# A hybrid decoder block on one core: memory keys ahead of the block, memory values inside its first feed-forward step, the memory output projection in token halves

## The chip, the cores and the metric

One core of a Trainium2 chip runs the whole kernel. The metric is device time in microseconds (us), median of several runs. Every matrix product outside the score and transpose steps is the sum of three fp32r products of operands split into a high and a low part.

## The reference

Sequence 1024, width 1024, feed-forward width 2816, 256 memory tokens, one layer.

```python
x = x + 0.5 * swiglu(rmsnorm(x, ffn1_norm), ffn1_w_gate, ffn1_w_up, ffn1_w_down)
x = x + hybrid_mixer(rmsnorm(x, mix_norm), ...)          # NSA and forgetting attention
x = x + memory_cross_attention(rmsnorm(x, mem_q_norm), rmsnorm(mem, mem_kv_norm), mem_w_q, mem_w_kv, mem_w_o)
x = x + 0.5 * swiglu(rmsnorm(x, ffn2_norm), ffn2_w_gate, ffn2_w_up, ffn2_w_down)
return rmsnorm(x, final_norm)
```

In the memory attention, `k, v = split(mem_n @ w_kv)`: keys and values depend on the memory alone, not on x. Its last step is `o @ w_o`.

## The kernel before

**The plan.** The kernel first describes all its work as operations with the engines that could do them and a cost in ns for each, and then `Plan.order` lays them out in one list: at each step it takes the engine on which something can start first and, among the operations that can start there within 60 ns of that, the one of lowest rank. An operation that names two engines goes to the one that is free first by the plan. The order in which operations come out is the order of each engine's instruction stream, and an engine takes its stream strictly in that order. So a cost in the plan changes no instruction; it changes what stands behind what. A rank is roughly the due time in us of TensorE's work (`self.r` grows by the cost of each TensorE operation); loads are ranked some us ahead of their use. Buffers come from shared pools (46 of 128x1024 in SBUF, 8 PSUM banks) with a cap per kind (`TAGS`: F 28, mT 4, raw weight sums' input wa 4, wf 6, results sg 4, vt 2, raw weight units wr 3, their two parts w 10, xs 3); the plan holds an operation back until a buffer is free by its own clock.

**Start.** `memory_kv` norms the two memory tiles (`norm_T`, buffers mT), then makes the eight key blocks (`keys`: one weight unit w each, one 256-column product in cc, stored to DRAM) and the two value halves (`values`: four weight units each, 512-column products, stored). A weight unit comes by DMA (wr), ScalarE casts its high part (L409), VectorE makes its low part (L413). All of it comes ahead of the first feed-forward step. The eight tiles of x (128 tokens each, tokens of the second half first: `late`) are normed at ranks 6 to 34 (`norm_forms`), between the keys and the values.

**A feed-forward step** uses a seven-product scheme for a two by two split of tokens and width (Winograd's). `Forms` holds the seven combinations of the normed, transposed x, each as high and low part (F). `norm_forms` norms a tile (square on ScalarE, reciprocal root on GpSimd, scale on VectorE in xn, L444), transposes it on TensorE (T, L381), copies it out (R for tokens of the second half, xs for the first, at most three xs at once), sums the parts a form needs (fs, L492, on GpSimd or VectorE) and splits it (L390 high, L397 low). Which form needs which (width half, token half) is said by

```python
SUMS = {1: ((0, 0), (1, 1), 1), 2: ((0, 0),), 3: ((0, 1), (1, 1), -1), 4: ((1, 0), (0, 0), -1), 5: ((1, 1),),
        6: ((0, 0), (0, 1), 1), 7: ((1, 0), (1, 1), 1)}
```

so forms 3 and 5 need tokens of the second half alone, 4 and 2 of the first half alone, and 1, 6 and 7 of both. `seven` makes the products in the order 3, 5, 4, 2, 1, 6, 7, each of 12 matmuls over 512 columns; `ffn_up` calls it for gate and up in each of 11 chunks, `left_sums` makes the weight sums (ws) and their split (wf). `ffn_down` follows.

**Second entry.** `out_proj("mo", ..., late=True)` makes the memory output projection for each half of the width (ch), and within it for all eight token tiles, second half first. Only with ch 1 is a tile of x complete: the add (L1327), then `done(t)`, which stores x and calls `norm_forms` for the second feed-forward step. A tile takes eight operations of 648 ns and two of 436 of TensorE's by the plan, so tiles stand 6.06 ranks apart.

## Time and profile before

| | us |
|---|---|
| median of 3 runs | 2586.99 (2584.11 to 2588.99) |
| profiled execution, its own time | 2588.4 |
| span of the trace in it | 2586.4 |
| TensorE busy | 2522.5 |
| VectorE busy | 1664.6 |
| ScalarE busy | 1180.9 |
| GpSimd busy | 619.3 |

The profiled execution is 1.4 us above the median, and 2.0 us of its time lie outside the span. Busy time is the union of an engine's instructions; times in rows are us from the start of the span, means of one instruction are ns.

### The profile page before, as it was taken

What the parts mean: (1) busy time and instruction counts of PE and PEld (TensorE: products, weight loads), DVE (VectorE), ACT (ScalarE), POOL (GpSimd) and SP (SyncE); (2) the same over time, 40 slices, a digit from 0 to 9 for tenths busy, and PEclk for the clock granted to TensorE, in tenths of its full rate; (3) what the DMA queues carried; (4) which work ended last, traced back from release to release, by engine and by line L of the source; (5) the groups of instructions that cost most, each with busy time, mean ns of one, the idle gap of its engine ahead of it and who ended that gap; (6) DMA issues with size and microseconds to landing.
All of it is one profiled execution on the core that took longest, in us unless ns stands there. A gap on an engine that the chain in (4) does not pass through costs nothing.

```text
span 2586.4 us, 34955 instructions
## 1 busy us (share of the span) xinstructions
PE 2522.5 (98%) x12613; PEld 2132.7 (82%) x12613; DVE 1664.6 (64%) x3120; ACT 1180.9 (46%) x2352; POOL 619.3 (24%) x590
## 2 busy tenths in 40 slices
PE   7899999999999999999999999999998999999998
PEld 6688888888788888898888888888876888888887
DVE  8755556667765477788766766344576556557566
ACT  6422232334445567777776753233443232233433
POOL 5643344331200001111000003000034334332313
PEclk9999999999999999999999999999998999999999
DMA  7233233696722110210212344241112223327964
GB/s 280 98 114 114 78 131 118 205 369 225 266 82 83 45 58 30 72 63 19 79 53 82 116 137 155 82 147 57 50 74 86 97 103 106 123 93 271 343 234 164
DMA packets 137485, 329.90 MB, mean 128 GB/s; under 512 B 14656, under 2 KB 18096, under 8 KB 137184
## 3 DMA queue, kind: packets, MB, share of 16 engines
q1 hardware_dynamic: 137248, 327.47, 36.5%
q8 instruction: 99, 1.62, 0.3%
q14 instruction: 74, 0.61, 0.1%
q0 software_dynamic: 64, 0.20, 0.0%
HBM read 254.17 MB, written 75.02 MB: 127 GB/s over the span
## 4 chain that ended last, share of the span: by engine, by line
PE 89%; DVE 3%; ACT 2%; DMA 1%; issue 1%; POOL 0%; SPq 0%; DVEq 0%; POOLq 0%; ACTq 0%
PE z L375 11%; PE z L376 11%; PE z L377 11%; PE mm L375 7%; PE mm L376 7%; PE mm L377 7%; PE y L376 5%; PE y L375 5%; PE y L377 5%; PE T L381 4%; PE pv L1124 4%; PE acc L377 2%; PE acc L375 2%; PE acc L376 2%; PE s L1049 2%; PE s L1050 2%
## 5 line engine op out<-in xcount | busy, mean ns | idle before, releaser
L375 PE MATMUL z<-F,wf 128*128 128x512 f32 x1232 | 483.1, 392 | 15.0 <-ACT wf L513 5.0
L377 PE MATMUL z<-F,wf 128*128 128x512 f32 x1232 | 482.0, 391 | 3.5 <-DVE wf L514 3.5
L376 PE MATMUL z<-F,wf 128*128 128x512 f32 x1232 | 482.6, 392 | 2.5 <-DVE F L397 2.4
L492 POOL TENSOR_TENSOR ws<-wa 128x512 f32<-128x512 f32 x197 | 285.7, 1465 | 507.6 <-DVE wf L514 333.6
L375 PEld LDWEIGHTS z<-F,wf 128*128 128x128 f32 x1232 | 232.8, 189 | 66.7 <-ACT wf L513 5.5
L375 PE MATMUL mm<-h,w 128*128 128x512 f32 x704 | 286.8, 407 | 0.0
L377 PE MATMUL mm<-h,w 128*128 128x512 f32 x704 | 276.5, 393 | 0.0
L376 PE MATMUL mm<-h,w 128*128 128x512 f32 x704 | 276.4, 393 | 0.0
L377 PEld LDWEIGHTS z<-F,wf 128*128 128x128 f32 x1232 | 232.7, 189 | 52.7 <-DVE wf L514 4.6
L376 PEld LDWEIGHTS z<-F,wf 128*128 128x128 f32 x1232 | 232.8, 189 | 52.2 <-DVE F L397 4.0
L376 PE MATMUL y<-df,gf 128*128 128x512 f32 x616 | 239.9, 389 | 1.1 <-DVE df L649 1.1
L375 PE MATMUL y<-df,gf 128*128 128x512 f32 x616 | 240.4, 390 | 0.0
L377 PE MATMUL y<-df,gf 128*128 128x512 f32 x616 | 239.9, 389 | 0.0
L514 DVE TENSOR_TENSOR wf<-ws,wf 128x512 fp32r<-128x512 f32 x220 | 170.7, 777 | 48.8 <-ACT wf L513 48.8
L397 DVE TENSOR_TENSOR pt<-T,pt 128x512 fp32r<-128x512 f32 (+1 forms) x264 | 156.2, 614 | 68.4 <-ACT pt L390 67.3
L390 ACT CAST pt<-T 128x512 fp32r<-128x512 f32 (+1 forms) x264 | 132.3, 528 | 77.5 <-PE T L381 75.5
L1077 ACT ACTIVATE p<-p,sm 128x128 f32<-128x128 f32 (+7 forms) x192 | 143.4, 747 | 46.3 <-DVE sm L1147 43.8
L377 PEld LDWEIGHTS mm<-h,w 128*128 128x128 f32 x704 | 132.6, 188 | 29.7
L513 ACT CAST wf<-ws 128x512 fp32r<-128x512 f32 x220 | 131.8, 619 | 47.4 <-PE z L377 45.5
L376 PEld LDWEIGHTS mm<-h,w 128*128 128x128 f32 x704 | 133.6, 190 | 18.8
L375 PEld LDWEIGHTS mm<-h,w 128*128 128x128 f32 x704 | 133.3, 189 | 19.0
L413 DVE TENSOR_TENSOR w<-wr,w 128x1024 fp32r<-128x1024 f32 x95 | 121.4, 1289 | 40.4 <-ACT w L409 38.7
(254 smaller groups left out, 5042.3 us busy)
## 6 DMA issues: line engine op xcount, KB each, us to landing
da<-in_w_dram SPq DMA_DIRECT2D x264, 256.0 KB, 5.9
wr<-in_w_dram SPq DMA_DIRECT2D x95, 512.0 KB, 4.7
wa<-in_w_dram SPq DMA_DIRECT2D x88, 512.0 KB, 3.9
dg<-gd SPq DMA_DIRECT2D x70, 512.0 KB, 6.0
gd<-gs SPq DMA_DIRECT2D x110, 256.0 KB, 2.1
xd<-x SPq DMA_DIRECT2D x24, 512.0 KB, 2.6
x<-xd SPq DMA_DIRECT2D x24, 512.0 KB, 5.9
gd<-sg SPq DMA_DIRECT2D x44, 256.0 KB, 2.1
```

What stands on the lines that cost most here:

```text
L375: mm(out, a[0], b[0], start=first, stop=False, skip_group_check=more)
L376: mm(out, a[0], b[1], start=False, stop=False, skip_group_check=more)
L377: mm(out, a[1], b[0], start=False, stop=last, skip_group_check=more)
L381: self.nc.tensor.transpose(out, src, self.ident[0:k, 0:k])
L390: nc.scalar.copy(h, s)
L397: nc.vector.tensor_sub(l, s, h.bitcast(F32))
L413: self.dve(1135, lambda: nc.vector.tensor_sub(lo(), raw(), hi().bitcast(F32)), [raw, hi], [lo], rank=r + 4)
L492: (nc.vector if en == "DVE" else nc.gpsimd).tensor_tensor(out(), a(), b(), op=op)
L513: self.act(512, lambda: nc.scalar.copy(w()[:, 0:512], val()), rd, [(w, 0)], sbuf=True, rank=rank + 3)
L514: self.dve(690, lambda: nc.vector.tensor_sub(w()[:, 512:1024], val(), w()[:, 0:512].bitcast(F32)), rd + [(w, 0)], [(w, 1)], rank=rank + 3)
L1077: nc.scalar.activation(p[e]()[:, 0:row[e]], p[e]()[:, 0:row[e]], AF.Exp, bias=m[e]()[:, j:j + 1], scale=-1.0, accum_out=l()[:, e:e + 1])
L1124: mm(pv()[:, 0:256], v, y()[:, b * 256:b * 256 + 256], start=unit["fresh"], stop=stop and y is lo)
```

## The change

It has five parts.

1. At the start the memory keys come first (ranks from -20), the loads and norms of x move forward among them (loads at ranks -13 to -2.5, norms at 3j-2), and the two value halves are moved into `ffn_up`, ahead of its third and fourth chunk. The low part of a key's weight unit may be made by VectorE or by GpSimd.
2. In `norm_forms` the sums and splits of forms 1, 6 and 7 get a rank 14 later (`WAIT`), in both feed-forward steps.
3. `out_proj("mo")` goes by token halves: tokens of the second half with both width halves, then tokens of the first half with both. The eight weight units are loaded and split twice.
4. In `norm_T` and `norm_forms` the plan counts the scale of a tile (xn) as ready 1000 ns later than it costs.
5. The plan's costs of VectorE operations on 512 columns go down from 690 to 603 ns (of `sum_on` and of the splits in `ffn_down` by 87 ns).

```diff
         if pool:
-            self.pool(2430, lambda: nc.gpsimd.tensor_sub(lo(), raw(), hi().bitcast(F32)), [raw, hi], [lo], rank=r + 4)
+            self.plan.op({"DVE": 1135, "POOL": 3000}, lambda en: (nc.vector if en == "DVE" else nc.gpsimd).tensor_sub(
+                lo(), raw(), hi().bitcast(F32)), [raw, hi], [lo], r + 4)
...
-            self.dve(1.042 * n + 130, scale, [x, st, g], [(out, key(j))])
+            self.dve(1.042 * n + 130, scale, [x, st, g], [(out, key(j))], delay=slack)
...
-        self.rms(x, g, xn)
+        self.rms(x, g, xn, slack=1000.0)
...
-        self.plan.op({"POOL": 2.9 * n + 50, "DVE": 1.04 * n + 157}, f, reads, writes, self.r if rank is None else rank)
+        self.plan.op({"POOL": 2.9 * n + 50, "DVE": 1.04 * n + 70}, f, reads, writes, self.r if rank is None else rank)
...
-            self.dve(690, lambda: nc.vector.tensor_sub(w()[:, 512:1024], val(), w()[:, 0:512].bitcast(F32)),
+            self.dve(603, lambda: nc.vector.tensor_sub(w()[:, 512:1024], val(), w()[:, 0:512].bitcast(F32)),
...
         for i in (5, 3) if half else (4, 2, 1, 6, 7):
-            parts = F.SUMS[i]
+            parts, rank = F.SUMS[i], self.r + (WAIT if i in (1, 6, 7) else 0.0)
...
-    def ffn_up(self, n, F):
+    def ffn_up(self, n, F, between={}):
...
         for c in range(H):
+            between.get(c, lambda: None)()
             sg = [self.buf("sg") for _ in range(2)]
...
-        g = self.gain("mem_kv_norm")
+        g = self.gain("mem_kv_norm", lead + 0.5)
...
-            w, ps, kt = self.weight(("mk", c)), self.buf("mm"), self.buf("cc", F32R)
+            w, ps, kt = self.weight(("mk", c), pool=True), self.buf("mm"), self.buf("cc", F32R)
...
-    def out_proj(self, name, y, x, done, late=False):
+    def out_proj(self, name, y, x, done, halves=(range(NT),)):
...
-        for ch in range(2):
+        for ts, ch in ((ts, ch) for ts in halves for ch in range(2)):
             ws = [self.weight((name, ch, j), 16.0 - 4 * j) for j in range(4)]
-            for t in [4, 5, 6, 7, 0, 1, 2, 3] if late else range(NT):
+            for t in ts:
...
-        for f in self.memory_kv(40.0):
+        self.r = -20.0
+        keys = self.memory_kv(0.0)
+        values = [keys.pop(), keys.pop()][::-1]
+        self.r = 0.0
+        for f in keys:
             f()
-        r = self.r
-        self.r = 2.0
-        g = self.gain("ffn1_norm", 0.0)
-        x = load(lambda t: io["x"][t], order=late, lead=2.0, step=2.0)
+        r, self.r = self.r, -13.0
+        g = self.gain("ffn1_norm", 0.5)
+        x = load(lambda t: io["x"][t], order=late, lead=0.0, step=1.5)
         F = Forms(self, "F")
         for j, t in enumerate(late):
-            self.r = 6.0 + 4.0 * j
+            self.r = 3.0 * j - 2.0
             self.norm_forms(x[t], g, F, t)
...
-        gd = self.ffn_up("1", F)
+        gd = self.ffn_up("1", F, {2: values[0], 3: values[1]})
...
-        self.out_proj("mo", o, x, done, late=True)
+        self.out_proj("mo", o, x, done, (late[:4], late[4:]))
...
-G0 = 3
+G0, WAIT = 3, 14.0
```

## Rows read from the trace of the kernel before

**Rows 1.** The page: span, busy time of TensorE (PE), and its granted clock in 40 slices of 64.7 us (tenths of full speed).

```profile
span 2586.4 us, 34955 instructions
...
PE 2522.5 (98%) x12613; PEld 2132.7 (82%) x12613; DVE 1664.6 (64%) x3120; ACT 1180.9 (46%) x2352; POOL 619.3 (24%) x590
...
PEclk9999999999999999999999999999998999999999
```

**Rows 2.** Who waited for whom, TensorE's waits alone, over the whole span (us in total, times, longest).

```profile
PE T L381 <- DVE xn L444: 26.0, 7, 8.1
PE z L375 <- ACT wf L513: 5.0, 1, 5.0
PE z L375 <- ACT vt L537: 4.3, 2, 3.7
```

**Rows 3.** Busy time of each engine in stretches of the start (us; in brackets the number of instructions; then granted clock, share of the DMA engines, GB/s).

```profile
0.00:18.30 18.30, 3.58 (x16) 3.18 (x17) 8.88 (x13) 10.16 (x17) 5.49 (x13) 1.00 0.91 339
18.30:60.00 41.70, 41.53 (x290) 38.94 (x288) 38.55 (x55) 32.73 (x69) 22.59 (x19) 1.00 0.76 271
60.00:110.00 50.00, 34.09 (x133) 26.22 (x134) 44.15 (x60) 26.02 (x59) 37.95 (x23) 0.90 0.29 102
```

**Rows 4.** Instructions of TensorE in order of time, first 110 us, those that waited longest (start us, us, line, what, count; in brackets the idle time before and what ended it).

```profile
16.68 1.97 PE L381 MATMUL T<-ident,xn 128*128 128x128 f32 x8 [6.61 <-DVE xn L444]
...
63.54 1.78 PE L381 MATMUL T<-ident,xn 128*128 128x128 f32 x8 [3.58 <-DVE xn L444]
79.68 1.94 PE L381 MATMUL T<-ident,xn 128*128 128x128 f32 x8 [5.22 <-DVE xn L444]
...
105.25 0.51 PE L375 MATMUL z<-F,wf 128*128 128x512 f32 x1 [2.02 <-DVE vt L541]
```

**Rows 5.** Groups of TensorE's instructions, first 110 us (busy us, mean ns of one | idle before). The memory keys are mm<-mT,w, the memory values mm<-w,mT, the feed-forward products z<-F,wf, the transposes of a normed tile T<-ident,xn; of the three lines L375, L376 and L377 of one product the first is shown.

```profile
L375 PE MATMUL mm<-mT,w 128*128 128x256 f32 x64 | 19.4, 303 | 0.0
L375 PE MATMUL mm<-w,mT 128*128 128x512 f32 x32 | 14.1, 439 | 0.0
L381 PE MATMUL T<-ident,xn 128*128 128x128 f32 x80 | 13.9, 331 | 23.5 <-DVE xn L444 23.5
L375 PE MATMUL z<-F,wf 128*128 128x512 f32 x23 | 9.4, 407 | 3.1 <-DVE vt L541 2.0 <-ACT vt L537 0.7 <-ACT F L390 0.4
```

**Rows 6.** Groups of VectorE's (DVE) instructions, first 105 us (busy us, mean ns of one | idle before).

```profile
L397 DVE TENSOR_TENSOR F<-fs,F 128x256 fp32r<-128x256 f32 x40 | 25.9, 700 | 1.6 <-ACT F L390 1.6
L413 DVE TENSOR_TENSOR w<-wr,w 128x1024 fp32r<-128x1024 f32 x16 | 21.9, 1381 | 2.9 <-ACT w L409 2.9
L444 DVE SCALAR_TENSOR_TENSOR xn<-x,sm,gain 128x1024 f32<-128x1024 f32 x8 | 13.6, 1702 | 0.0
L397 DVE TENSOR_TENSOR cc<-mm,cc 128x256 fp32r<-128x256 f32 (+1 forms) x11 | 5.3, 486 | 1.4 <-ACT cc L390 1.4
```

**Rows 7.** Busy time of each engine in two stretches at the entry to the second feed-forward step (columns as in group 3).

```profile
1927.80:1962.00 34.20, 20.36 (x64) 14.80 (x62) 26.61 (x44) 16.54 (x42) 18.00 (x13) 0.75 0.17 62
1962.00:1996.00 34.00, 34.00 (x152) 28.15 (x151) 22.07 (x30) 9.06 (x17) 9.75 (x8) 1.00 0.26 89
```

**Rows 8.** Instructions of TensorE in order of time at the same place, those that waited.

```profile
1934.46 0.80 PE L375 MATMUL z<-F,wf 128*128 128x512 f32 x1 [3.67 <-ACT vt L537]
1944.00 0.80 PE L375 MATMUL z<-F,wf 128*128 128x512 f32 x1 [5.03 <-ACT wf L513]
1952.94 0.50 PE L375 MATMUL z<-F,wf 128*128 128x512 f32 x1 [3.23 <-ACT F L390]
1955.25 0.80 PE L376 MATMUL z<-F,wf 128*128 128x512 f32 x1 [1.80 <-DVE F L397]
```

**Rows 9.** Instructions of VectorE in order of time: the last split of a form at the start, and then at the second entry.

```profile
95.83 2.47 DVE L397 TENSOR_TENSOR F<-fs,F 128x256 fp32r<-128x256 f32 x2 [1.62 <-ACT F L390]
...
1925.90 6.06 DVE L397 TENSOR_TENSOR F<-fs,F 128x256 fp32r<-128x256 f32 x8
...
1938.53 2.76 DVE L397 TENSOR_TENSOR F<-fs,F 128x256 fp32r<-128x256 f32 x8
1941.22 0.68 DVE L1327 TENSOR_TENSOR x<-acc,x 128x512 f32<-128x512 f32 x1
...
1944.59 1.28 DVE L444 SCALAR_TENSOR_TENSOR xn<-x,sm,gain 128x1024 f32<-128x1024 f32 x1
```

**Rows 10.** Instructions of GpSimd (POOL) in order of time at the same place.

```profile
1924.87 2.27 POOL L492 TENSOR_TENSOR fs<-xs,R 128x512 f32<-128x512 f32 x1 [0.66 <-DVE F L397]
1927.84 1.42 POOL L492 TENSOR_TENSOR fs<-xs,R 128x512 f32<-128x512 f32 x1 [0.70 <-DVE F L397]
1929.61 1.40 POOL L492 TENSOR_TENSOR fs<-xs 128x512 f32<-128x512 f32 x1 [0.36 <-DVE F L397]
```

**Rows 11.** Busy time of each engine in a dense stretch of the first feed-forward step.

```profile
250.00:300.00 50.00, 50.00 (x222) 41.39 (x222) 28.47 (x41) 15.43 (x29) 23.20 (x16) 1.00 0.34 121
```

**Rows 12.** Busy time of each engine while the memory output projection runs, and TensorE's only wait of that stretch.

```profile
1840.00:1889.00 49.00, 48.44 (x219) 39.96 (x218) 16.20 (x18) 8.27 (x11) 2.04 (x3) 1.00 0.06 22
...
1888.05 1.09 PE L381 MATMUL T<-ident,xn 128*128 128x128 f32 x8 [0.56 <-DVE xn L444]
```

**Rows 13.** Groups over the whole span with shapes kept apart: a subtraction or sum of 128x1024 on GpSimd, and the cast of a weight unit on ScalarE (ACT).

```profile
L409 ACT CAST w<-wr 128x1024 fp32r<-128x1024 f32 x95 | 98.9, 1053 | 79.2 <-PE acc L377 53.0 <-DMA wr<-in_w_dram 15.3 <-DVE w L413 6.7
...
L492 POOL TENSOR_TENSOR da<-da 128x1024 f32<-128x1024 f32 x24 | 66.0, 2750 | 178.7 <-DMA da<-in_w_dram 114.9 <-DVE df L649 46.6 <-PE z L376 8.7
```

More of the change, by code (lines that the diff above doesn't have):

```diff
@@ L360, in act, with dve @@
                      hold=hold)
-    def dve(self, ns, run, reads, writes, rank=None):
-        self.plan.op({"DVE": ns}, lambda _: run(), reads, writes, self.r if rank is None else rank)
+    def dve(self, ns, run, reads, writes, rank=None, delay=0.0):
+        self.plan.op({"DVE": ns}, lambda _: run(), reads, writes, self.r if rank is None else rank, delay)
     def pool(self, ns, run, reads, writes, rank=None):
@@ L421, in gain, with rms @@
         return g
-    def rms(self, x, g, out, parts=1):
+    def rms(self, x, g, out, parts=1, slack=0.0):
         nc, n = self.nc, D // parts
@@ L540, in seven @@
         product(4, y, True)
-        self.dve(690, lambda: nc.vector.tensor_add(v(), y(), v()), [y], [(vt, 0)])
+        self.dve(603, lambda: nc.vector.tensor_add(v(), y(), v()), [y], [(vt, 0)])
         product(2, y, False)
@@ L544, in seven @@
         product(1, x, True)
-        self.dve(690, lambda: nc.vector.tensor_add(v(), x(), v()), [x], [(vt, 0)])
+        self.dve(603, lambda: nc.vector.tensor_add(v(), x(), v()), [x], [(vt, 0)])
         product(6, y, False)
-        self.dve(690, lambda: sub(d, y), [y, (vt, 0)], [(vt, 1)])
+        self.dve(603, lambda: sub(d, y), [y, (vt, 0)], [(vt, 1)])
         use(1, 1, d, [(vt, 1)])
         product(7, z, False)
-        self.dve(690, lambda: sub(v, z), [z], [(vt, 0)])
+        self.dve(603, lambda: sub(v, z), [z], [(vt, 0)])
         use(0, 0, v, [(vt, 0)])
@@ L556, in norm_forms @@
         xn = self.buf("xn")
-        self.rms(x, g, xn)
+        self.rms(x, g, xn, slack=1000.0)
         raw = F.raw[t] = self.buf("R" if half else "xs")
@@ L577, in norm_forms @@
                 s = self.buf("fs")
-                self.sum_on(512, s, lambda parts=parts: part(parts[0]), lambda parts=parts: part(parts[1]), parts[2], src, [s])
+                self.sum_on(512, s, lambda parts=parts: part(parts[0]), lambda parts=parts: part(parts[1]), parts[2], src, [s], rank)
                 val, rd = s, [s]
@@ L582, in norm_forms @@
             self.split(512, view, lambda p=put: p(0), lambda p=put: p(1), rd, [(b, t % 4) for b in F.t[i][0]],
-                       [(b, t % 4) for b in F.t[i][1]], count=2, sbuf=True)
-    def ffn_up(self, n, F):
+                       [(b, t % 4) for b in F.t[i][1]], count=2, sbuf=True, rank=rank)
+    def ffn_up(self, n, F, between={}):
         nc, H = self.nc, NFF // 2
@@ L598, in up @@
             def up(i, j, view, reads, sg=sg, at=at):
-                self.dve(690, lambda: nc.vector.tensor_mul(at(i, j), at(i, j), view()), reads, [(sg[i], j)])
+                self.dve(603, lambda: nc.vector.tensor_mul(at(i, j), at(i, j), view()), reads, [(sg[i], j)])
             self.seven(("g" + n, c), ("g" + n, c + H), F, gate)
@@ L648, in load @@
                          rank=r + 3, hold=[hl[1]])
-                self.dve(1.04 * w + 157, lambda b=b, hl=hl: nc.vector.tensor_sub(
+                self.dve(1.04 * w + 70, lambda b=b, hl=hl: nc.vector.tensor_sub(
                     hl[1]()[:, 0:w], b()[:, 0:w], hl[0]()[:, 0:w].bitcast(F32)), [b, hl[0]], [hl[1]], rank=r + 3)
@@ L679, in f @@
                 stt(xs, bank[t](), xs, s)
-            self.dve(690, f, [bank[t]], [(x[tb], ch)])
+            self.dve(603, f, [bank[t]], [(x[tb], ch)])
         def plus_v(t, tb, ch):
@@ L686, in ffn_down @@
         y2 = [self.buf("y") for _ in range(4)]
-        stage(3, z, True, lambda t: self.dve(690, lambda: stt(v(t), z[t](), v(t), 0.5), [z[t]], [vk(t)]))
-        stage(4, y2, True, lambda t: self.dve(690, lambda: stt(v(t), y2[t](), v(t), 0.5), [y2[t]], [vk(t)]))
+        stage(3, z, True, lambda t: self.dve(603, lambda: stt(v(t), z[t](), v(t), 0.5), [z[t]], [vk(t)]))
+        stage(4, y2, True, lambda t: self.dve(603, lambda: stt(v(t), y2[t](), v(t), 0.5), [y2[t]], [vk(t)]))
         x.extend(self.load_x(range(8)))
```

## The prediction

> **What bounds the kernel.** I read the page first. TensorE is busy for 2522.5 us of a span of 2586.4 [rows 1], and no edit adds or removes a matmul. So the change can only act through the 63.9 us in which TensorE stands, and through the stretches where its granted clock is below full. Then the busy time by stretches: in the first 110 us TensorE stands 14.7, 0.2 and 15.9 us, 30.8 in all [rows 3]; in the 34.2 us after 1927.8, where the second feed-forward step begins, 13.8 [rows 7]. That leaves 19.3 us elsewhere, its end included.
>
> A stand costs more than itself, because the clock falls with it. From 60 to 110 us TensorE issues 133 matmuls: 69 of the feed-forward products (3 x 23), 16 transposes, and so 48 for the memory values [rows 3, 5]. In a dense stretch 222 matmuls over 512 columns take 50 us, 0.225 each [rows 11]; 117 of them take 26.3 us and the transposes some 1.8, so 28.1 of the 50 us are work and **21.9 are lost**, at a granted clock of 0.90. From 1927.8 to 1962.0 there are 53 product matmuls (11.9 us) and 11 transposes (some 1.1): 13.0 of 34.2 are work, **21.2 lost**, at a granted clock of 0.75, which is part of the stretch at 1.2 GHz instead of 2.4 [rows 7].
>
> Who is late is read from the waits and the order of time. TensorE's largest wait by name is for normed tiles, 26.0 us in seven waits [rows 2]: 8.1, 6.61, 3.58 and 5.22 of it at the start [rows 2, 4], 2.5 elsewhere. VectorE is behind that: from 60 to 110 us it is busy 44.15 of 50 [rows 3]. At the second entry the reader is to look at one instruction: the add that completes the last tile of x runs at 1941.22, though TensorE's last product for it ended before 1927.8. It stands behind splits of forms (eight in 6.06 us, eight in 2.76) [rows 9], and TensorE waits through four gaps of 3.67, 5.03, 3.23 and 1.80 us for what follows [rows 8].
>
> **Part 2 and 3 at the second entry.** Before, the sums and splits of a tile's five forms share its rank, so those of the earlier tiles rank ahead of the last tile's add. With 14 added, forms 1, 6 and 7 of the two tiles before the last rank behind the last tile's add, norm and forms 4 and 2 (tiles are about 6 ranks apart, so only the first of the four, 18 ahead, stays ahead by 4). The add can then run at about 1928. From the add to the second matmul of product 4 the trace has 1941.22 to 1955.25, 14.0 us [rows 8, 9], with transposes waiting behind matmuls in it; so product 4 can start between 1939 and 1942. TensorE has products 3 and 5 of gate and of up until then, 48 matmuls or 10.8 us: to 1939.6 with a tile's transposes. Next late would be forms 1, 6 and 7. VectorE did 26.6 us of work in the 34.2 [rows 7]; without its 7.6 us of idle time that ends at about 1954, while TensorE with products 4 and 2 of both is busy to 1950 and with 1 and 6 to 1961. I leave 5 us lost of 21.2 (bounds 2 and 13): **-16**.
>
> Going by token halves (part 3) puts the norms of the first four tiles a quarter of the projection earlier, so VectorE has no backlog from them when the last four come. Its price: eight more weight units, VectorE 8 x 1.38 = 11.0 us and ScalarE 8 x 1.05 = 8.4 [rows 6, 13], and 4 MB more by DMA. They are hidden by a stretch in which VectorE is busy 16.2 of 49 us and the DMA engines 0.06 [rows 12]. Each of the two added changes of weight units is covered by the matmuls of the tile before; at the one change there is already, near 1887, TensorE waits 0.56 us, and that for a normed tile [rows 12]. Without cover a change costs a cast and a low part, 1.05 + 1.38 = 2.4 us, 4.9 for two. I take 0.
>
> **Part 1 and 2 at the start.** The 96 matmuls of the values, 21.6 us, leave the start and come back in the third and fourth chunk. They do not get cheaper, so the start gains only if the feed-forward products come more than 21.6 us earlier. TensorE's side: it is busy 41.53 us from 18.3 to 60 [rows 3], 10.8 of it 48 value matmuls, so keys and six tiles' transposes take 30.7, with two more tiles about 33: they end at 51. Before, the 48 matmuls of the first four products were out at 105.25 [rows 4]; now they could be out at 51 + 10.8 = 61.8. Against 105.25 - 21.6 = 83.65 this is at best 21.9 us, just what is lost there today. VectorE's side: the values take half of the 16 low parts, 10.95 us, and some 2 us of the cc splits with them [rows 6], so its last form, ready at 95.83 + 2.47 = 98.3 before [rows 9], is ready at about 85. Forms 1, 6 and 7 are 24 of the 40 F<-fs splits, 15.5 us, and some sums; deferred, they leave forms 3, 5, 4, 2 ready at about 68. TensorE comes to product 4 at about 62 (products 3 and 5 of both), waits some 6 us, is busy with 4 and 2 of both to 79, and meets form 1 at 76, 6 at 81, 7 at 85. With a lower clock after the gap I leave 11 us lost of 21.9: **-11**. Bounds: 0 lost (-21.9), or no faster VectorE at all (rival 3). The first 18.3 us stay: the second memory tile still follows several loads.
>
> The low parts of the keys on GpSimd or VectorE: no row shows this operation on GpSimd. The nearest is a two-operand one of the same size there, 2.75 us [rows 13], against 1.38 on VectorE [rows 6]. Bounds: eight saved on VectorE, -11 us for it, or eight that hold it up for 2.75 each, +11. VectorE's splits show which is near: eight take 2.76 us beside an idle GpSimd and 6.06 while three sums run there, of which 4.1 us fall inside [rows 9, 10]. I take 0.
>
> That slowdown is what the Trainium skill states (SBUF — State Buffer, section "SBUF: two separate sides"): a VectorE operation with two SBUF inputs and a reading GpSimd operation exclude one another for the whole instruction. The trace agrees: 3.3 us more for 4.1 us of sums. By that rule the choice of GpSimd helps nothing, which is a rival below.
>
> **The values inside the step.** They bring TensorE their 21.6 us, already counted. VectorE gets 13 us more in some 75; it is busy 28.5 of 50 there, ScalarE 15.4, the DMA engines 0.34 [rows 11]: hidden, 0. What is not free is SBUF room: 28 buffers of F and four of mT leave 14 of 46, where the step may use up to 16 for weights, sums and results, and each value weight takes three more. If none of the eight units is prefetched, each costs 2.4 us, 19 in all; if all are, 0. Three raw units may be held at once, so nearer 0: **+2**.
>
> **Parts 4 and 5.** They change no instruction. Counting xn as later puts more matmuls ahead of transposes; outside the two entries there are 2.5 us of such waits to win. New costs reshuffle order everywhere; elsewhere TensorE stands 19.3 us, part of it behind its last matmul where no order helps; half of it, some 10 us, is the most that could go, and a worse order could cost as much. I take **-1**.
>
> **Sum.** -16 - 11 + 2 - 1 = -26 against the profiled execution's 2588.4 (span 2586.4 and 2.0 around it): 2562.4. That execution was 1.4 above the median of the runs, so 2561 for the median.
>
> **Rivals.**
> 1. The sum as it stands, 2561, its own range 2547 to 2572: chance 0.55.
> 2. Only the second entry gains. At the start TensorE catches up with VectorE and stands as long as before: 2561 + 11 = 2572. For it: VectorE is busy 38.55 of 41.7 us even before 60 [rows 3]. Against it: 13 us of its work leave. 0.20.
> 3. On the other side: the values were cover. If VectorE delivers no sooner, the first four products still end at 105.25, TensorE stands 21.6 us more, and the start costs +21.6 instead of -11: 2561 + 32.6 = 2594. It decides from a ready time of 83.65 for the start alone, and of about 99 for the whole change. For it: VectorE is the busy engine there. 0.07.
> 4. Room: casts and sums of the third and fourth chunk wait for buffers, 14 us beyond my 2: 2575. 0.07.
> 5. The order hardly changes (the plan already thought TensorE gapless, real lateness returns elsewhere): 2587. The waits of [rows 8] would stay, only with other names. 0.06.
> 6. GpSimd takes most low parts of the keys and holds VectorE up as long as it saves, +11 on VectorE: the start's gain is gone, 2572. For it: the 6.06 against 2.76 [rows 9]; against it: the plan takes GpSimd only where it is free first. 0.05. This is the rule named above.
>
> **Range and chances.** About 5 us (0.2%) is what these runs can tell from no change. Cases 1, 2, 4 and 6 are faster by more: 0.87. Case 5: same, 0.06. Case 3: slower, 0.07. The range goes from both entries near their floor (-21.9, -19, no cost inside the step: 2547) to a little past cases 2, 4 and 6: 2579; left out are cases 3 and 5 and a tail of case 1.
>
> **What would show it.** Right: the first four feed-forward products are out between 62 and 80 us; mm<-w,mT stands somewhere between 115 and 200 us with TensorE at 50 of 50; the last x<-acc add runs within 2 us of its last product, and the 34 us after it hold some 120 to 150 matmuls instead of 64; waits T<-xn fall from 26.0 to under 20. Wrong: the first four products out later than 84 us; TensorE waits on w or wf between 115 and 200; gaps of over 3 us at the second entry, then for forms 1, 6 or 7; a VectorE as long behind with GpSimd busy on the keys' low parts.

## The result, and the profile after

The changed kernel takes 2601.91 us (median; 2600.26 to 2605.11) where the kernel before takes 2585.59 in the same comparison: a ratio of 1.0063, 95% interval 1.0045 to 1.008. It is slower by 16 us; forecast were 26 less. The profiled execution after has 2600.26, span 2598.4, against 2588.4 and 2586.4 before [rows 1], so the traces show 12.0 of the 16: the execution profiled before lay 2.8 above the median of its kernel's runs in this comparison, the one after 1.6 below.

The page after, span and busy time. TensorE's work is the same, 2523.0 us, so the loss is time in which it stands.

```profile
span 2598.4 us, 34997 instructions
...
PE 2523.0 (97%) x12613; PEld 2130.1 (82%) x12613; DVE 1691.6 (65%) x3135; ACT 1186.4 (46%) x2350; POOL 613.6 (24%) x593
```

The busy times by stretches of the start (columns as in [rows 3]). TensorE stands 14.4, 7.2 and 13.4 us, 34.9 against 30.8 before. VectorE has one us of the last 50 free; before, 5.9.

```profile
0.00:18.30 18.30, 3.94 (x16) 3.14 (x16) 6.32 (x11) 10.32 (x19) 9.07 (x15) 1.00 0.88 343
18.30:60.00 41.70, 34.55 (x246) 32.96 (x247) 39.60 (x49) 28.74 (x65) 29.90 (x25) 1.00 0.55 203
60.00:110.00 50.00, 36.58 (x147) 27.90 (x146) 48.98 (x66) 23.32 (x54) 26.72 (x19) 0.90 0.17 57
```

The second entry, the 34.2 us from the end of the last projection product and the 34.2 after it (as [rows 7]). The first hold 64 TensorE instructions, the number of before, at the same granted clock of 0.75; and VectorE, 26.61 busy before, now has no idle moment.

```profile
1935.00:1969.20 34.20, 17.84 (x64) 12.68 (x62) 34.20 (x47) 15.67 (x39) 21.40 (x16) 0.75 0.19 62
1969.20:2003.40 34.20, 33.51 (x148) 27.73 (x149) 21.00 (x31) 9.35 (x17) 9.98 (x8) 1.00 0.21 73
```

To see where 12 us come from I cut each trace at three events in TensorE's own order: the start of its 1100th matmul, transposes not counted (by then all these kernels have made the keys, the values and the same number of feed-forward products), the end of the last product of the memory output projection, and the start of the 97th product matmul of the second feed-forward step. The 480th matmul is one more mark in the start; in the changed kernel all but 12 of the 96 value matmuls lie behind it. Each row is one execution.

| kernel (median us) | 480th | start: to 1100th | middle | second entry | end |
|---|---|---|---|---|---|
| before (2585.6) | 137.8 | 278.4 | 1648.8 | 44.8 | 614.4 |
| after (2601.9) | 144.8 | 288.2 | 1646.7 | 46.0 | 617.4 |
| e1_start_old (2588.4) | 134.7 | 275.2 | 1647.9 | 46.0 | 616.2 |
| f1_values_at_start (2593.1) | 139.4 | 279.9 | 1650.0 | 44.9 | 617.3 |
| f2_two_m (2603.2) | 144.8 | 287.6 | 1651.4 | 46.0 | 617.3 |
| h3_keys_low_vector (2599.0) | 142.5 | 285.6 | 1649.9 | 46.0 | 616.2 |
| e2_sums_vector (2585.2) | 139.9 | 283.0 | 1646.9 | 37.3 | 616.2 |
| e3_before_sums_vector (2574.2) | 131.4 | 271.9 | 1646.9 | 38.9 | 614.3 |
| h1_sums_and_rank (2574.4) | 137.4 | 277.9 | 1642.6 | 37.8 | 614.4 |
| g3_before_halves_sums (2572.8) | 132.2 | 272.7 | 1646.2 | 38.1 | 614.3 |
| f4_best (2579.6) | 133.5 | 274.0 | 1647.8 | 38.2 | 616.2 |
| g2_best_old_costs (2573.3) | 134.5 | 275.0 | 1644.6 | 37.8 | 614.3 |
| e6_old_costs (2594.2) | 144.4 | 287.5 | 1644.4 | 45.5 | 614.6 |
| k1_before_new_costs (2584.7) | 136.5 | 277.0 | 1647.9 | 41.5 | 616.9 |
| g1_before_sums_gpsimd (2582.6) | 138.2 | 278.7 | 1645.5 | 41.7 | 614.7 |
| e4_wait0 (2601.8) | 149.4 | 292.3 | 1652.1 | 40.7 | 616.2 |

So +9.8 at the start (forecast -11 and +2), +1.2 at the second entry (forecast -16), -2.1 in the middle and +3.0 behind it (forecast -1). The middle differs by up to 10 us among these kernels, and two things in the traces account for it. TensorE's clock is at its lower level, 1.2 GHz, for nothing of it (after, h1) up to 6.8 us, which costs up to 3.4; and TensorE's waits there add up to between 8.4 us (h1) and 13.8 (e4). Without both, all sixteen middles lie between 1633.6 and 1635.4. So totals that differ by a few us are read by their columns.

### The profile page after: what moved, and what is told of

Same layout as the page of the kernel before. It is cut to its first block, busy times and chain, and to the rows that moved or that the text cites. A ratio compares the mean times of both kernels' runs of the same rounds, so it can differ in the third digit from the quotient of the medians.

```text
span 2598.4 us, 34997 instructions
## 1 busy us (share of the span) xinstructions
PE 2523.0 (97%) x12613; PEld 2130.1 (82%) x12613; DVE 1691.6 (65%) x3135; ACT 1186.4 (46%) x2350; POOL 613.6 (24%) x593
## 4 chain that ended last, share of the span: by engine, by line
PE 66%; DVE 4%; ACT 1%; issue 1%; DMA 1%; SPq 0%; POOL 0%; DVEq 0%; POOLq 0%; ACTq 0%
PE mm L375 7%; PE mm L376 7%; PE mm L377 7%; PE z L375 5%; PE z L377 5%; PE z L376 5%; PE T L381 4%; PE pv L1126 4%; PE y L376 3%; PE y L377 3%; PE y L375 3%; PE acc L376 2%; PE acc L377 2%; PE acc L375 2%; PE s L1051 2%; PE s L1052 2%
## 5 line engine op out<-in xcount | busy, mean ns | idle before, releaser
L375 PE MATMUL z<-F,wf 128*128 128x512 f32 x1232 | 483.9, 393 | 18.6 <-ACT vt L538 7.3
L377 PE MATMUL z<-F,wf 128*128 128x512 f32 x1232 | 482.2, 391 | 9.4 <-DVE wf L515 9.4
L376 PE MATMUL z<-F,wf 128*128 128x512 f32 x1232 | 482.4, 392 | 2.3 <-DVE F L397 2.3
L493 POOL TENSOR_TENSOR ws<-wa 128x512 f32<-128x512 f32 x194 | 278.9, 1452 | 485.9 <-DVE wf L515 302.3
L375 PEld LDWEIGHTS z<-F,wf 128*128 128x128 f32 x1232 | 232.9, 189 | 71.5 <-ACT vt L538 8.8
L375 PE MATMUL mm<-h,w 128*128 128x512 f32 x704 | 286.0, 406 | 0.0
L377 PEld LDWEIGHTS z<-F,wf 128*128 128x128 f32 x1232 | 232.8, 189 | 59.0 <-DVE wf L515 10.5
L377 PE MATMUL mm<-h,w 128*128 128x512 f32 x704 | 275.9, 392 | 0.0
L376 PE MATMUL mm<-h,w 128*128 128x512 f32 x704 | 275.8, 392 | 0.0
L376 PEld LDWEIGHTS z<-F,wf 128*128 128x128 f32 x1232 | 232.8, 189 | 51.5 <-DVE F L397 3.8
L376 PE MATMUL y<-df,gf 128*128 128x512 f32 x616 | 240.1, 390 | 2.0 <-DVE df L651 2.0
L377 PE MATMUL y<-df,gf 128*128 128x512 f32 x616 | 240.0, 390 | 0.5 <-DVE gf L651 0.5
L375 PE MATMUL y<-df,gf 128*128 128x512 f32 x616 | 240.3, 390 | 0.0
L1079 ACT ACTIVATE p<-p,sm 128x128 f32<-128x128 f32 (+7 forms) x192 | 143.4, 748 | 46.1 <-DVE sm L1149 43.7
L377 PEld LDWEIGHTS mm<-h,w 128*128 128x128 f32 x704 | 132.2, 188 | 29.4
L376 PEld LDWEIGHTS mm<-h,w 128*128 128x128 f32 x704 | 133.0, 189 | 19.0 <-DVE h L397 0.3
L375 PEld LDWEIGHTS mm<-h,w 128*128 128x128 f32 x704 | 132.8, 189 | 18.8
```

The lines of the kernel that those rows point to most:

```text
L375: mm(out, a[0], b[0], start=first, stop=False, skip_group_check=more)
L376: mm(out, a[0], b[1], start=False, stop=False, skip_group_check=more)
L377: mm(out, a[1], b[0], start=False, stop=last, skip_group_check=more)
L493: (nc.vector if en == "DVE" else nc.gpsimd).tensor_tensor(out(), a(), b(), op=op)
L1079: nc.scalar.activation(p[e]()[:, 0:row[e]], p[e]()[:, 0:row[e]], AF.Exp, bias=m[e]()[:, j:j + 1], scale=-1.0, accum_out=l()[:, e:e + 1])
```

## The experiments

All are given with their ratio to the kernel before, 95% interval in brackets. My theory after the result: VectorE's work, lengthened by what GpSimd does beside it, sets both entries, so its order is worth little, and the memory values were what TensorE did meanwhile. The rival: the new order itself is bad, at one of its places.

**Which of the parts costs. e1_start_old** undoes part 1.

```diff
...
-        self.r = -20.0
-        keys = self.memory_kv(0.0)
-        values = [keys.pop(), keys.pop()][::-1]
...
+        for f in self.memory_kv(40.0):
             f()
...
-            self.r = 3.0 * j - 2.0
+            self.r = 6.0 + 4.0 * j
...
-        gd = self.ffn_up("1", F, {2: values[0], 3: values[1]})
+        gd = self.ffn_up("1", F)
```

> Part 1 undone: memory keys and values ahead of the block as before, ranks, loads and GpSimd choice of the keys' low parts as before; parts 2 to 5 kept. Theory that the values were cover (VectorE sets when the forms are ready, TensorE has 21.6 us less to do meanwhile): the last split of a form at the start comes no later than 100 us, the 505th product matmul back near 209 us instead of 218, and the time about 9 to 10 us below the changed kernel, 2592. Rival, that the loss comes from the new costs and ranks (parts 2, 4, 5): the start stays late and the time stays within 3 us of 2602.

Measured: 2588.36, 1.0011 (1.0002 to 1.002). Part 1 costs 13.5 us, 13.0 of them in the start column; parts 2 to 5 together gain 3.2 at the start and lose 1.2 and 1.8 at the second entry and the end.

**f1_values_at_start** leaves part 1 but puts the values back behind the keys.

```diff
-        values = [keys.pop(), keys.pop()][::-1]
+        values = []
...
-        gd = self.ffn_up("1", F, {2: values[0], 3: values[1]})
+        gd = self.ffn_up("1", F)
```

> The changed kernel with the memory values back behind the keys, ahead of the first feed-forward step; its loads, ranks and choice of engine for the keys' low parts stay. Cover theory (the values filled TensorE while VectorE made the forms): most of part 1's 13 us come back, the 505th product matmul near 208, time 2590 to 2594. Rival (the later start of the keys, 25.6 against 18.3 us, and the keys' low parts on GpSimd cost it): no more than 4 us come back, 2598 or more.

Measured: 2593.08, 1.003 (1.002 to 1.004). The move of the values costs 8.8 us. By the columns it is 8.3: 5.4 by the 480th matmul, where the values are missing as cover, and 2.9 behind it, around the values inside the step. There TensorE stands while a weight unit's low part is made, as this line of the trace after shows:

```profile
165.65 0.50 PE L376 MATMUL mm<-w,mT 128*128 128x512 f32 x1 [1.22 <-DVE w L414]
```

**h3_keys_low_vector** takes GpSimd from the low parts of the keys.

```diff
-            w, ps, kt = self.weight(("mk", c), pool=True), self.buf("mm"), self.buf("cc", F32R)
+            w, ps, kt = self.weight(("mk", c)), self.buf("mm"), self.buf("cc", F32R)
```

> The changed kernel with all eight low parts of the keys on VectorE (of which it had four on GpSimd at about 2.5 us each). Rival 6 says that GpSimd holds VectorE up for as long as it saves: then within 2 us of the changed kernel's 2601.9, last form of the start within 2 us of 105.6. If the low parts on GpSimd cost more than they save (2.5 us of hold-up against 1.4 of work, four times): 2596 to 2599. If they saved their work: 2605 or more.

Measured: 2598.99, 1.0047 (1.0032 to 1.0062), 2.6 us less at the start; its interval and that of the changed kernel overlap. The last form is ready at 97.8 instead of 105.6. VectorE's groups of the first 105 us, after and then in this kernel, show why:

```profile
L397 DVE TENSOR_TENSOR F<-fs,F 128x256 fp32r<-128x256 f32 x40 | 26.7, 716 | 0.5 <-ACT F L390 0.5
L515 DVE TENSOR_TENSOR wf<-ws,wf 128x512 fp32r<-128x512 f32 x8 | 8.2, 1024 | 0.0
L397 DVE TENSOR_TENSOR F<-R,F 128x256 fp32r<-128x256 f32 x8 | 7.6, 988 | 0.0
L397 DVE TENSOR_TENSOR F<-xs,F 128x256 fp32r<-128x256 f32 x8 | 6.9, 916 | 0.0
L411 DVE TENSOR_TENSOR w<-wr,w 128x1024 fp32r<-128x1024 f32 x4 | 5.9, 1485 | 0.0
L515 DVE TENSOR_TENSOR wf<-wa,wf 128x512 fp32r<-128x512 f32 x4 | 4.6, 1141 | 0.0
...
L397 DVE TENSOR_TENSOR cc<-mm,cc 128x256 fp32r<-128x256 f32 x8 | 3.3, 408 | 0.0
...
L414 DVE TENSOR_TENSOR w<-wr,w 128x1024 fp32r<-128x1024 f32 x1 | 1.2, 1211 | 0.0
```

```profile
L397 DVE TENSOR_TENSOR F<-fs,F 128x256 fp32r<-128x256 f32 x40 | 23.9, 648 | 0.0
...
L414 DVE TENSOR_TENSOR w<-wr,w 128x1024 fp32r<-128x1024 f32 x8 | 12.9, 1614 | 0.0
...
L397 DVE TENSOR_TENSOR F<-xs,F 128x256 fp32r<-128x256 f32 x8 | 7.4, 958 | 0.0
...
L397 DVE TENSOR_TENSOR F<-R,F 128x256 fp32r<-128x256 f32 x8 | 3.0, 410 | 0.0
```

GpSimd made four of the keys' low parts. That saved VectorE 7.0 us of them (12.9 against 5.9; the single 1.2 is a value's) and cost it 6.9 in the same 56 splits of forms (41.2 against 34.3); F<-R alone went from 410 to 988 ns. The norms went the other way, 13.5 us after and 15.3 here.

**f2_two_m** lets both memory tiles be loaded at once, since the keys start late (25.6 us after, 18.3 before).

```diff
-    "kc": ("u", 4), "flat": ("u", 2), "fl": ("u", 4), "mT": ("u", 4), "m": ("u", 1),
+    "kc": ("u", 4), "flat": ("u", 2), "fl": ("u", 4), "mT": ("u", 4), "m": ("u", 2),
```

> The changed kernel with two buffers for the raw memory tiles in the plan, so that the second memory tile is loaded right behind the first. Both theories have the keys start some 6 us sooner, before 20 us. Cover theory: VectorE still sets when the forms are ready, so the 505th product matmul moves by less than 3 us and the time stays at 2599 to 2603. Rival (the late keys cost it): it moves by the same 6 us, time 2596 or less.

Measured: 2603.24, 1.0063 (1.0048 to 1.0078). The keys start 11.5 us sooner, at 14.1, and the 1100th matmul comes 0.6 sooner. The late keys cost nothing. The last form is ready at 96.7, 8.9 us sooner than after, and the 480th matmul comes when it did. Of the 13.0 us of part 1 in the start column 8.3 are thus the values and 2.6 the keys' low parts; some 2 are left to the earlier x, if the parts add.

**What sets the entries. e3_before_sums_vector** is the kernel before with one edit: the sums of `norm_forms` on VectorE alone. Before, six of the 20 at the start and eight of the 20 at the second entry ran there.

```diff
-    def sum_on(self, n, out, a, b, sign, reads, writes, rank=None):
+    def sum_on(self, n, out, a, b, sign, reads, writes, rank=None, only=None):
...
-        self.plan.op({"POOL": 2.9 * n + 50, "DVE": 1.04 * n + 157}, f, reads, writes, self.r if rank is None else rank)
+        on = {"POOL": 2.9 * n + 50, "DVE": 1.04 * n + 157}
+        self.plan.op({e: c for e, c in on.items() if only in (None, e)}, f, reads, writes, self.r if rank is None else rank)
...
-                self.sum_on(512, s, lambda parts=parts: part(parts[0]), lambda parts=parts: part(parts[1]), parts[2], src, [s])
+                self.sum_on(512, s, lambda parts=parts: part(parts[0]), lambda parts=parts: part(parts[1]), parts[2], src, [s], only="DVE")
```

> The kernel before with the sums of norm_forms on VectorE alone, nothing else. Port theory: 5 to 15 us faster than before, 2570 to 2581. Rival (VectorE full): 14 sums more at the start and 9 at the second entry, about 14 us slower, 2600.

Measured: 2574.16, 0.9961 (0.9946 to 0.9975): 10.5 us faster than before, 6.5 at the start and 5.9 at the second entry (12.4 in all: the execution of before that was profiled lies 3.7 above the median here). VectorE has 26 sums more, and over the whole span it is busy as long as before, 1665.2 us against 1664.6. Three views of this kernel: VectorE's groups in the first 105 us, its instructions in order of time at the second entry, and the 34.2 us there by engine (as [rows 7]).

```profile
L397 DVE TENSOR_TENSOR F<-fs,F 128x256 fp32r<-128x256 f32 x40 | 17.6, 485 | 0.6 <-ACT F L390 0.5
L444 DVE SCALAR_TENSOR_TENSOR xn<-x,sm,gain 128x1024 f32<-128x1024 f32 x8 | 10.2, 1274 | 0.0
L492 DVE TENSOR_TENSOR fs<-xs,R 128x512 f32<-128x512 f32 x12 | 9.1, 773 | 0.0
```

```profile
1926.33 0.68 DVE L492 TENSOR_TENSOR fs<-xs,R 128x512 f32<-128x512 f32 x1
...
1927.60 2.76 DVE L397 TENSOR_TENSOR F<-fs,F 128x256 fp32r<-128x256 f32 x8
1930.28 0.67 DVE L1328 TENSOR_TENSOR x<-acc,x 128x512 f32<-128x512 f32 x1
```

```profile
1918.90:1953.10 34.20, 24.68 (x92) 18.61 (x91) 25.24 (x52) 17.59 (x44) 12.69 (x8) 0.80 0.19 62
```

Against [rows 6] the 40 splits fall from 25.9 to 17.6 us and the norms from 13.6 to 10.2. Eight splits take 2.76 us, and the last tile's add comes 11.4 us after its last product instead of 14.1. The window holds 92 TensorE instructions where before and after hold 64. At the second entry 30 splits are left after the last projection product, of 412 ns each; before 33 of 609, after 34 of 762. The sums of `norm_forms` on GpSimd in that time were none, six and nine, the weight sums there two, three and five. The edit takes two things away together, the longer splits and the wait for sums that GpSimd makes late; no run separates them.

**e2_sums_vector** does the same to the changed kernel, with the keys' low parts on VectorE too (both edits are shown above).

> The changed kernel with the sums of norm_forms (20 in each feed-forward step) and the keys' low parts on VectorE alone. Port theory (GpSimd's operations stretch VectorE's splits from 0.41 to 0.8 or 1.0 us, and each sum moved saves up to 1.4 of blocking and costs 0.6): splits of forms at 0.41 to 0.5 us in the mean, both entries shorter by 3 to 10 us, time 2585 to 2597. Rival (VectorE is simply full, whatever GpSimd does): 13 sums more for it at the start and 14 at the second entry, 0.6 us each, both entries longer by 8, time about 2618.

Measured: 2585.22, 1.0001 (0.9991 to 1.001), 16.7 us below the changed kernel: 8.7 at the second entry, 5.2 at the start. The cover that the values were stays lost: its start column is 11.1 above that of e3.

**g1_before_sums_gpsimd** puts those sums on GpSimd alone (`only="POOL"`) in the kernel before.

> The kernel before with the sums of norm_forms on GpSimd alone, the opposite step: 6 sums leave VectorE at the start and 11 at the second entry. Port theory: each blocks VectorE for up to 1.4 us instead of costing it 0.6, and comes late besides, so 3 to 15 us slower than before. Rival (VectorE is simply full): 17 x 0.6 us less for it, 5 to 10 us faster.

Measured: 2582.63, 0.9987 (0.9977 to 0.9996), where I had expected a loss. The splits after the last product take 811 ns each, longer than anywhere, and yet the second entry is 3.1 us shorter than before; VectorE has no sums of its own there, which may offset the splits, but that is not shown. This kernel does not give the reference's output, so I build nothing more on it.

**h1_sums_and_rank** adds part 2 to e3.

```diff
+            parts, rank = F.SUMS[i], self.r + (WAIT if i in (1, 6, 7) else 0.0)
...
-G0 = 3
+G0, WAIT = 3, 14.0
```

> The kernel before, with the sums of norm_forms on VectorE alone (as e3_before_sums_vector, 2574.2 us) and part 2: the later rank for forms 1, 6 and 7. With GpSimd silent beside the splits, this asks what the order alone is worth. If the order helps once the splits are short (my theory of the prediction, with its cause of failure taken away): the add of the last tile comes within 7 us of the last product instead of 11.4, and the time is 2570 or less. If the total of VectorE's work sets the entry whatever its order: 2574 within 3. If the rank hurts (f4_best had parts 2 to 5 and 2579.6): 2577 to 2580.

Measured: 2574.44, 0.9956 (0.9939 to 0.9972), the time of e3. The add of the last tile comes 6.3 us after its product instead of 11.4, and the second entry is 1.1 shorter; the start is 6.0 longer, its last form ready at 103.9 against 95.3. The order alone moves the entries in opposite directions. The total equals that of e3 only through the middle, which is 4.3 shorter: 3.4 of it because this trace has no stretch at 1.2 GHz there, where that of e3 has 6.8 us.

**g3_before_halves_sums** adds part 3 to e3.

```diff
-        self.out_proj("mo", o, x, done, late=True)
+        self.out_proj("mo", o, x, done, (late[:4], late[4:]))
```

> The kernel before, with the sums of norm_forms on VectorE alone and part 3: the projection by token halves, its eight more weight units. If the units are hidden, as the prediction had them at 0, and the halves bring nothing when VectorE is not held up: 2574 within 3. If the halves help VectorE's backlog: the last split nearer to the last product, 2570 or less. If part 3 carries the 5 us that f4_best lost against e3_before_sums_vector: 2577 to 2580.

Measured: 2572.76, 0.9948 (0.9933 to 0.9963): 1.4 less than e3, inside the interval of either. The eight more weight units are hidden, and they buy nothing that can be told from nothing.

**e4_wait0** is the changed kernel with `WAIT = 0.0`.

> Part 2 undone (no later rank for forms 1, 6 and 7), all else as in the changed kernel. If the later rank brings the last add forward as I forecast but the gain is given back behind it: the add falls back to some 14 us behind its last product, the 97th product matmul of the step stays about 45 us behind it, time within 3 us of 2602. If bunched sums of the late forms beside the splits cost more than the order gains: 5 us faster. If the later rank does help: 5 to 10 us slower.

Measured: 2601.75, 1.0065 (1.005 to 1.008), the time of the changed kernel, with a start 4.1 longer and a second entry 5.3 shorter. This kernel does not give the reference's output either, and no conclusion rests on it. So with the sums on both engines no run shows what part 2 alone is worth.

**The planner's costs. f4_best** is parts 2 to 5 with the old start, as e1, and the sums on VectorE; **g2_best_old_costs** is f4 with part 5 undone; of its eleven lines two stand here.

```diff
-        on = {"POOL": 2.9 * n + 50, "DVE": 1.04 * n + 70}
+        on = {"POOL": 2.9 * n + 50, "DVE": 1.04 * n + 157}
...
-        self.dve(603, lambda: sub(v, z), [z], [(vt, 0)])
+        self.dve(690, lambda: sub(v, z), [z], [(vt, 0)])
```

> Parts 2 to 5 of the change with the start of before, and the sums of norm_forms on VectorE alone. Port theory: against the same kernel with the sums on either engine (2588) it gains 8 to 14 us, 2574 to 2580. If parts 2 to 5 are worth something once VectorE is not held up, it goes below the kernel before with its sums on VectorE: under 2572. If they cost what they cost with the sums on both engines, 2578.

> f4_best (parts 2 to 5, the old start, norm_forms' sums on VectorE; 2579.6 us) with part 5 undone: the planner's old, higher costs of VectorE. If the lower costs make a plan that puts too much on VectorE or counts on it too early: 2574 to 2577. If they only reshuffle: 2579.6 within 2.

Measured: 2579.63, 0.9976 (0.9966 to 0.9986), and 2573.32, 0.995 (0.9935 to 0.9965). With e3, h1, g3 and g2 within 2 us of one another, parts 2, 3 and 4 bring no gain once the sums are on VectorE: against e3, g2 has a start 3.1 longer, a second entry 1.1 shorter and a middle 2.3 shorter. Part 5 costs 6.3 there, 4.6 in the two traces, of it 3.2 in the middle and 1.9 at the end.

**e6_old_costs** undoes part 5 in the changed kernel, **k1_before_new_costs** gives it to the kernel before, by the same lines.

> The changed kernel with part 5 alone undone: the planner's old, higher costs of VectorE. If the lower costs take 6 us here too, as between f4_best and g2_best_old_costs: 2595 to 2597, with the wait y<-df in the second step's projection (1.5 us) gone. If they only cost when VectorE carries all the sums of norm_forms: 2602 within 2.

> The kernel before with part 5 alone: the lower costs. e1_start_old (parts 2 to 5) stood 2.8 us above before. If part 5 carries that: 2588 to 2591, and parts 2, 3 and 4 together are worth nothing or less. If part 5 is harmless with the sums mixed: 2585.6 within 2, and the loss of e1_start_old is that of parts 2 to 4.

Measured: 2594.19, 1.003 (1.0019 to 1.0042), and 2584.72, 0.9995 (0.9985 to 1.0004). Part 5 costs 7.7 us in the changed kernel and nothing in the kernel before. One part of it is the same everywhere: in the second step's down projection TensorE waits once for a difference that VectorE makes. The line is from k1, from 2360 us on:

```profile
PE y L376 <- DVE df L649: 1.5, 1, 1.5
```

All nine kernels with the lower costs have this wait of 1.5 to 1.6 us, none of the other seven has it, and their end columns are 616.2 to 617.4 against 614.3 to 614.7. In k1 that is paid back by 3.3 at the second entry. The traces of after and e6 show 6.4 of the 7.7: 2.8 at the end, 2.3 in the middle, where TensorE's waits add up to 11.3 us instead of 8.6, 0.7 at the start and 0.5 at the second entry. Why the lower costs order the middle worse stays open.

## Why the prediction was wrong, point by point

**What bounds the kernel** held in the main: the work of TensorE is unchanged, 11.0 of the 12 us lie in the start and the second entry, and VectorE is the engine behind them. The 3.0 behind the second entry were not foreseen. Of the signs named, the 34 us hold 64 matmuls as before, and the waits T<-xn are 22.0 us, not under 20.

**The second entry, -16; it came to +1.2.** The add was moved as said, if less: 6.8 us after its last product (1934.96 to 1941.77) instead of 14.1 [rows 9], not within 2. The step that failed is "VectorE did 26.6 us of work in the 34.2; without its 7.6 us of idle time that ends at about 1954". The idle time did go, but the work grew by as much: 34.2 us busy, the last split at 1969.2. The splits left were as many as before, 34 for 33, but GpSimd had nine sums of `norm_forms` in that stretch instead of six and five weight sums instead of three, and the splits went from 609 to 762 ns: 5.8 of the 7.6 us. I had seen eight splits take 6.06 us beside GpSimd and 2.76 elsewhere [rows 9, 10], and used it for the keys' low parts only, not for the work whose end I forecast. I also misread the 2.76: GpSimd was not idle beside them. A sum overlaps them, and there it was the sum that took long (GpSimd, before):

```profile
1939.42 3.00 POOL L492 TENSOR_TENSOR ws<-wa 128x512 f32<-128x512 f32 x1 [3.64 <-DVE F L397]
```

Instructions of after in order of time, VectorE's and then GpSimd's:

```profile
1957.43 2.89 DVE L397 TENSOR_TENSOR F<-xs,F 128x256 fp32r<-128x256 f32 x2
1960.24 0.75 DVE L397 TENSOR_TENSOR F<-fs,F 128x256 fp32r<-128x256 f32 x2
1960.91 0.68 DVE L515 TENSOR_TENSOR wf<-wa,wf 128x512 fp32r<-128x512 f32 x1
```

```profile
1957.18 2.85 POOL L493 TENSOR_TENSOR fs<-xs,R 128x512 f32<-128x512 f32 x2
1961.13 1.59 POOL L493 TENSOR_TENSOR ws<-wa 128x512 f32<-128x512 f32 x1 [1.10 <-DVE F L397]
```

Two splits beside two sums take 2.89 us, as long as the sums; two in the gap between GpSimd's instructions take 0.75. The Trainium skill says so (SBUF — State Buffer, section "SBUF: two separate sides"): a VectorE operation with two SBUF inputs and a GpSimd operation that reads SBUF exclude each other for a whole instruction, and the trace agrees, 2.89 for 0.75.

A second step failed too: "TensorE has products 3 and 5 of gate and of up until then, 48 matmuls or 10.8 us: to 1939.6". In the plan's order gate's products 4, 1, 2, 6 and 7 stand ahead of up's 5 and of the second half of up's 3. So the first 48 product matmuls are gate's 3, 5 and 4 with half of up's 3 and half of gate's 1; the copy of up's product 3 runs only at 1981.15. They end at 1968.8. And "Next late would be forms 1, 6 and 7" does not hold here: none of TensorE's waits there is for a form; they are for other things queued behind them. Its three longest waits, then ScalarE's instructions:

```profile
1945.37 0.79 PE L375 MATMUL z<-F,wf 128*128 128x512 f32 x1 [6.43 <-ACT vt L538]
1957.09 0.80 PE L375 MATMUL z<-F,wf 128*128 128x512 f32 x1 [6.00 <-ACT wf L514]
1961.64 0.80 PE L377 MATMUL z<-F,wf 128*128 128x512 f32 x1 [3.33 <-DVE wf L515]
```

```profile
1942.47 1.06 ACT L434 ACTIVATE xn<-x 128x1024 f32<-128x1024 f32 x1 [1.44 <-DVE x L1330]
...
1943.53 1.31 ACT L390 CAST F<-fs 128x256 fp32r<-128x256 f32 x4
1944.74 0.57 ACT L538 COPY vt<-z 128x512 f32<-128x512 f32 x1
...
1955.20 0.71 ACT L390 CAST F<-xs 128x256 fp32r<-128x256 f32 x2 [4.14 <-DVE xs L569]
1955.82 0.71 ACT L390 CAST F<-fs 128x256 fp32r<-128x256 f32 x2
1956.43 0.61 ACT L514 CAST wf<-wa 128x512 fp32r<-128x512 f32 x1
...
1981.15 0.59 ACT L538 COPY vt<-z 128x512 f32<-128x512 f32 x1
```

Read backwards: the matmul at 1957.09 waits for the cast of a weight block wf (1956.43). ScalarE could have made it sooner, but in its stream it stands behind casts of a form (1955.20) that wait 4.14 us for a copy that VectorE makes late, behind its splits. The low part of that block is the 0.68 us at 1960.91 shown above, again behind splits, and TensorE waits 3.33 for it. The copy of a product's result (1944.74) stands behind the square of the last tile, which waits for the add. Of the waits of [rows 8] the two longest kept their names and grew (vt 6.43 us for 3.67, wf 6.00 for 5.03); those for forms gave way to 3.33 for wf and 1.05 for vt. That is close to rival 5, stands that return elsewhere.

How much each step carries, e2 shows. Without the sums of `norm_forms` on GpSimd the second entry of the changed kernel takes 37.3 us: 8.7 of the 17.2 that the forecast missed come back. The other 8.5 do not; there TensorE waits for a form at its 25th product matmul (3.37 us), where the prediction had work for 48. And against e3, which has the old order, e2 is only 1.6 shorter.

**Part 3 at 0** was right in its price. While the projection runs, VectorE is busy about twice as long in this window as in [rows 12] (in 83 us of the projection 51.7 against 45.9), and TensorE stands nowhere:

```profile
1840.00:1889.00 49.00, 49.00 (x229) 40.74 (x228) 31.58 (x44) 21.23 (x36) 4.09 (x7) 1.00 0.29 96
```

What it should have bought, a VectorE without backlog, it did not buy (g3).

**The start, -11; it came to +7.0 by the 480th matmul.** The failed step is the time at which VectorE has the forms ready: "forms 3, 5, 4, 2 ready at about 68" and the last form at "about 85". VectorE's last sum for form 4 ends at 80.0, and the last form is ready at 105.6; before, at 98.3. What I subtracted did leave in the first 105 us: 14.8 us of low parts (21.9 to 7.1) and 2.0 of the values' splits. What I left out came in: the 56 form splits, 31.9 us before [rows 6, for 25.9 of them], took 41.2, and 6.9 of these 9.3 us go when GpSimd makes no low parts (h3); the low parts of the step's weight blocks wf, which now are made earlier, went from eight in 8.0 us to twelve in 12.8; and some five us of sums and copies. So the list of what VectorE does until then was too short, and its durations were those of the kernel before. TensorE's instructions that waited, after:

```profile
78.36 0.79 PE L377 MATMUL z<-F,wf 128*128 128x512 f32 x1 [6.02 <-DVE wf L515]
...
98.32 0.49 PE L375 MATMUL z<-F,wf 128*128 128x512 f32 x1 [1.77 <-ACT F L390]
100.34 0.51 PE L376 MATMUL z<-F,wf 128*128 128x512 f32 x1 [1.52 <-DVE F L397]
104.22 0.50 PE L376 MATMUL z<-F,wf 128*128 128x512 f32 x1 [0.83 <-DVE F L397]
```

The first is among the first four products, which in the plan's order are gate's 3 and 5, up's 3 and gate's 4 and not 3 and 5 of both; it waits for a low part of wf that VectorE makes behind splits; these products are out at 86.3, where the prediction put the limit at 83.65. Six of the value matmuls (1.4 us) stand before that after all, so 1.3 us were lost there. The others are in gate's products 6 and 7, where the last forms are late; behind the first four products 5.7 more were lost.

That the last form came 7.3 us later than before and the 480th matmul 7.0 does not show that the one sets the other. In f2 and h3 the last form is ready 8.9 and 7.8 us sooner than after, and the 480th matmul comes 0.0 and 2.3 sooner. In f2 TensorE waits for earlier forms instead, 8.51 us at 72.21 and 4.79 at 77.80. It takes the forms one by one in the order of its stream, and a forecast needs the time of each. What the runs show for the loss are the values (f1) and, less surely, the keys' low parts (h3).

**Inside the step, +2** was measured as 2.8, from the 480th to the 1100th matmul (143.4 us against 140.6).

**Parts 4 and 5, -1.** Part 4 was not run alone; no run needs it to explain anything. For part 5 "a worse order could cost as much" as 10 us was the right bound and -1 the wrong value: 7.7 in the changed kernel, 6.3 with the sums on VectorE, nothing in the kernel before.

**The rivals.** Rival 3 is the nearest: the values were cover, and its point of decision for the whole change, a last form at about 99, is passed by the measured 105.6, though f2, with 96.7, loses as much. Its price was not what I wrote: the first four products did come 18.9 us sooner, and f1 gives 8.8 us for the move of the values where I had 21.6. What took it past 2594 is the second entry, which rival 3 still counted as won. Rival 6 holds for the splits in h3, 6.9 us of hold-up for 7.0 saved, but not for the time of the last form: without GpSimd it comes 7.8 us sooner, where rival 6 has no change. That GpSimd cost more than it saved is what 2.6 us at the start suggest; 2.9 in the medians are too few to show it. I had it as an alternative to rival 3, but both delay VectorE's forms, and they can add.

## What to carry to other kernels

Work of one engine that fills its wait for another is not loss to be moved away: it pays to move it only by as much as the other engine's results come sooner, so forecast these times first, one by one in the order in which the stream takes them, with every instruction in the queue, down to the small ones of the next stage. Cost VectorE's two-input work at what it takes beside GpSimd, not alone; giving GpSimd a share of it can save nothing, and here one edit that took GpSimd's sums away (e3) was worth 10.5 us where the whole reordering cost 16. And where a wait keeps its name after a reorder, look for what stands ahead of it in the same stream; read the order of the products from the plan, and do not assume it.

## What the runs showed of the hardware

The hold-up was larger than I had thought, and it falls on one side or the other. In the trace after, splits of a form from a sum (F<-fs) take 0.41 us when no GpSimd instruction overlaps them (42). Of the 38 that one overlaps, 17 take 0.41 to 0.58 all the same and 21 take 1.42 to 1.52, about as long as a sum. The scale of a norm likewise takes 1.27 to 1.29 us or, four times, 2.3 to 3.5. Where VectorE's splits keep their pace, the sum beside them is the one that takes long: 3.00 us in before beside eight splits in 2.76, and 3.01 in e3. cc<-mm, which takes one input from PSUM, isn't touched: 0.41 us with a GpSimd instruction beside it (four, at the start) and without (four). At the second entry a sum of 512 columns on GpSimd takes 1.27 to 2.25 us. And a low part of 128x1024, which no row of before showed on GpSimd, takes 2.51 us there against 1.21 on VectorE alone:

```profile
L411 POOL TENSOR_TENSOR w<-wr,w 128x1024 fp32r<-128x1024 f32 x4 | 10.0, 2510 | 2.3 <-ACT w L409 2.3
```
